# Where a weight piece begins in its buffer, against the activations that stream past it

## The chip, the cores and the metric

One core of a Trainium2 chip runs the whole program. The metric is the time of one execution on the device, in microseconds (us); the smaller the better. TensorE (PE in the profile) does two things for each matmul: it loads a stationary block of 128x128 values (LDWEIGHTS, the row PEld) and then streams the moving operand past it (MATMUL, the row PE). Both operands lie in the on-chip memory SBUF, where each tile has a byte address that is the same in all 128 partitions.

## The reference

Two transformer-like blocks on 256 tokens of width 2048, in float32. The first puts 16 meta tokens ahead, so its first projection works on 272 columns.

```
# first block
proj = rms(h) @ w_in                       # 2048 -> 10704
y_a  = rwkv7(...); y_b = fox_attention(...)
h = h + (g_a * (y_a @ w_a) + g_b * (y_b @ w_b)) @ w_o
h = h + (silu(gate) * up) @ w_down         # gate, up = rms(h) @ w_gate_up, width 5632
# second block
proj = rms(h) @ w_in_2                     # hyena and latent attention
h = h + rms(concat(rms(y_hyena), rms(y_attn)) @ w_out_2)
h = h + rms((gelu(conv3(g)) * u) @ w_down_2)   # g, u = rms(h) @ w_up_2, width 5632
```

## The kernel before

Every dense layer keeps its activations transposed in SBUF, 128 features by 256 (or 272) tokens for each of its k blocks, as two tiles: a high part (`xh`, in the chip's rounded float32 form) and the rest (`xl`). Weights come from memory in **pieces**: 8 blocks of 128x128, 4096 bytes in each partition. `weights` fetches a piece on the SP queue into `wr`, ScalarE writes its high part `wh` (line 191), VectorE the rest `wl` (line 192). `wr`, `wh` and `wl` rotate over three buffers each. `stream` hands out the blocks of a weight matrix piece by piece; `dense` takes one per k block and `mm3` issues three matmuls for it: `wh` by `xh` (L209), `wl` by `xh` (L210), `wh` by `xl` (L211). With a k depth of 16 a result takes two pieces, with 44 (`w_down`) five and a half. Piece numbers below count from 0 within a stream.

A scheduler orders each engine's instructions ahead of time from a simulated timeline; the order is fixed when the program is built. The stages follow each other:

| stage | matmuls stream | us in the profile |
|---|---|---|
| `w_in` with the RWKV and attention heads between | xh, xl | 0 to 801 |
| `w_ab` (`phase_merge`) | yah, yal, ybh, ybl | 801 to 916 |
| `w_o` | mh, ml | 916 to 1017 |
| `w_gu` (`phase_glu`) | x2h, x2l | 1017 to 1504 |
| `w_down` | hh, hl | 1504 to 1753 |
| `w_in2`, `w_q2`, `w_k2`, hyena, attention (`phase_mix`) | x3h, x3l; hyh, hyl; huh, hul | 1753 to 2013 |
| `w_out2` (`phase_out`) | yhh, yhl, yah2, yal2 | 2013 to 2113 |
| `w_up2` (`phase_conv_glu`) | x4h, x4l | 2113 to 2609 |
| `w_down2` (`phase_last`) | the weights, 512 columns at a time | 2609 to 2866 |

From `w_ab` through `w_o` the small matmuls of the hyena filters (dh, dl by flsh, flsl, fldh, fldl) and some float32 ones stand between the dense ones; in `phase_mix` those of hyena and attention do.

**Addresses.** The text speaks of the *distance* of a matmul: the byte address of its weight block less that of the block that it streams, modulo 256. A block of weights is 512 bytes and a block of 256 tokens 1024 bytes, so within a stage the distance is the same for all matmuls of a piece; in `w_in` a block of 272 tokens is 1088 bytes, and the distance goes down by 64 from one k block to the next. The addresses are those of the built program: `wh` at 40736, 44832, 48928 and `wl` at 53024, 57120, 61216 (all 32 modulo 256); xh 106912 (160), yah 65376 (96), mh 180192 (224), x2h, x3h and x4h 65376 (96), hh 122848 (224), yhh 194528 (224). `shift` allocates a tile of 64 bytes that nobody reads, so that the tiles behind it begin 64 bytes later.

Some pieces come apart from the others: `away` names pieces that `stream` puts in a pool of their own (tiles `awh`, `awl`), at another distance: 2, 6, 40 and 100 of `w_gu` and 10, 14, 48 and 100 of `w_up2` have distance 0, and 2 of `w_down` has 128. The filters' matmuls (dh, dl) have distance 0 throughout.

Of the kernel before, what the change touches and what calls it, by code (L numbers as in the profile page):

```python
# [12 lines left out]
F32R = mybir.dt.float32r  # L13
# [5 lines left out]
P = 128  # L19
D = 2048  # L20
KT = D // P
S = 256
# [6 lines left out]
HT = HID // P  # L29
C0 = math.exp(-0.5)  # L30
BIG = 1e30
PIECE = 8


# [48 lines left out]
CML, NCML = layout([("perm", 128), ("cos", S), ("sin", S)])  # L83
# [67 lines left out]
class Builder:  # L151
# [41 lines left out]

    def weights(self, src, kt, pools=None, size=PIECE, tag="w"):

        nc = self.nc
        praw, phi, plo = pools or (self.wraw, self.whi, self.wlo)
        w = self.tl(praw, [P, size, P], "wr")
        wh = self.tl(phi, [P, size, P], tag + "h", F32R)
        wl = self.tl(plo, [P, size, P], tag + "l", F32R)  # L200
        with self.tc.high_priority(offset=2000):
            nc.sync.dma_start(out=w[:, :kt], in_=src)
            self.split(w[:, :kt], wh[:, :kt], wl[:, :kt])
        return wh, wl
# [7 lines left out]

    def shift(self, pool):

        self.tl(pool, [P, 16], "shift")

    def stream(self, name, away=(), pool=None):


        w = self.a[name]  # L220
        for i in range(w.shape[0]):
            if i in away:
                wh, wl = self.weights(w[i], PIECE, (self.wraw, pool[0], pool[0]), tag="aw")
            else:
                wh, wl = self.weights(w[i], PIECE)
            for k in range(PIECE):
                yield wh[:, k], wl[:, k]
# [78 lines left out]
    def run(self):  # L306
# [16 lines left out]
        with ExitStack() as right:  # L323
# [15 lines left out]
            with ExitStack() as pb:  # L339
                xp = self.pool(pb, "x2")  # L340
                self.shift(xp)
                xh = self.tl(xp, [P, KT, S], "x2h", F32R)
                xl = self.tl(xp, [P, KT, S], "x2l", F32R)
                st = self.stream("w_o")
                for i in range(KT):
                    ps = self.bank()
                    self.dense(ps, st, KT, mh, ml, al)
                    self.residual(i, ps, "n2", xh, xl)
                    next(filters, None)
                pf.close()  # L350
                pm.close()
                self.rstd(self.R[:, :S], self.total(self.acc), S, 1.0 / D, 1e-6)
                self.dump("h1", self.h)
                pd = ExitStack()
                hp = self.pool(pd, "hp", side="right")
                hh = self.tl(hp, [P, HT, S], "hh", F32R)
                hl = self.tl(hp, [P, HT, S], "hl", F32R)
                self.phase_glu(xh, xl, hh, hl)
            with ExitStack() as pc:
                xp = self.pool(pc, "x3")  # L360
                self.shift(xp)
                xh = self.tl(xp, [P, KT, S], "x3h", F32R)
                xl = self.tl(xp, [P, KT, S], "x3l", F32R)
                with ExitStack() as c:
                    st = self.stream("w_down", (2,), [self.pool(c, "pdn")])
                    for i in range(KT):
                        ps = self.bank()
                        self.dense(ps, st, HT, hh, hl, al)
                        self.residual(i, ps, "pre", xh, xl)
                        if i % 4 == 3:  # L370
                            nc.scalar.dma_start(out=spill[:, i - 3 : i + 1], in_=self.h[:, i - 3 : i + 1])
                pd.close()
                self.dump("h2", self.h)
                ph.close()
                self.rstd(self.R[:, :S], self.total(self.acc), S, 1.0 / D, 1e-6)
                py = ExitStack()
                yp = self.pool(py, "yp", side="right")
                ys = [self.tl(yp, [P, 8, S], n, F32R) for n in ("yhh", "yhl", "yah2", "yal2")]
                rs = [self.tl(yp, [P, S], n) for n in ("Rh", "Ra")]
                self.phase_mix(xh, xl, ys, rs)  # L380
            with ExitStack() as pe:
                xp = self.pool(pe, "x4")
                self.shift(xp)
# [12 lines left out]
                self.phase_conv_glu(xh, xl, hh, hl, bring, spill2, pf)  # L396
                self.dump("h3", self.h)
# [111 lines left out]
    def phase_merge(self, pa, mh, ml, filters):  # L509
        nc, a = self.nc, self.a  # L510
        al = slice(0, S)
        w = self.pool(pa, "pmgy")
        self.shift(w)
        w2 = self.pool(pa, "pmg", 2)
# [4 lines left out]
        for j, k in ((0, 2), (2, 2), (4, 2), (6, 2)):  # L519
            for sp, yh, yl in ys:  # L520
                y = self.tl(w, [P, 2, S], "yraw", bufs=2)
                with self.tc.high_priority(offset=1500):
                    nc.gpsimd.dma_start(out=y, in_=sp[j : j + k].rearrange("j p s -> p j s"))
                    self.split(y, yh[:, j : j + k], yl[:, j : j + k])
        st = self.stream("w_ab")
        self.banks = "dac"
# [20 lines left out]
    def phase_glu(self, xh, xl, hh, hl):  # L547
# [3 lines left out]
        with ExitStack() as c:  # L551
            st = self.stream("w_gu", (2, 6, 40, 100), [self.pool(c, "pgl")])
            w2 = self.pool(c, "pglu", 2)
            for i in range(HT):
                ps = self.bank()
# [24 lines left out]
    def phase_mix(self, xh, xl, ys, rs):  # L580
# [3 lines left out]
        with ExitStack() as c:  # L584
# [7 lines left out]

            win2 = self.stream("w_in2")

# [53 lines left out]
            for q in range(2):  # L648
                wh, wl = self.weights(a["w_v2"][q], PIECE)
                wh, wl = (x.rearrange("p (k x) c -> p k (x c)", k=2) for x in (wh, wl))  # L650
                for b in range(2):
# [6 lines left out]
                    nc.scalar.copy(vt[:, b, 512 * q : 512 * q + 512], ps)  # L658
            acca = self.tl(w, [P, S], "acca")
            acch = self.tl(w, [P, S], "acch")  # L660
            hyena = self.hyena(w, w2, inproj, ys, acch)
            for h in range(8):
# [13 lines left out]
                for b in range(2):  # L676
                    nc.vector.tensor_scalar(out=sc[:, b], in0=sc[:, b], scalar1=sm[:, b : b + 1], scalar2=None, op0=ALU.mult)
                    for s_ in range(2):
                        nc.tensor.transpose(pT[:, s_, b], sc[:, b, 128 * s_ : 128 * s_ + 128], self.con("ident"))
                pt = self.tl(w, [P, 2, 2, P], "mpt")  # L680
                nc.scalar.copy(pt, pT)
# [191 lines left out]
    def phase_conv_glu(self, xh, xl, hh, hl, bring, spill, pf):  # L873
# [3 lines left out]
        with ExitStack() as c:  # L877
            pool = []
            st = self.stream("w_up2", (10, 14, 48, 100), pool)
            first = [self.bank() for _ in range(4)]  # L880
# [4 lines left out]
            pf.close()  # L885
            pool.append(self.pool(c, "pcgw"))
            w2 = self.pool(c, "pcg", 2)
# [68 lines left out]
    def phase_x(self, pa):  # L956
# [4 lines left out]
        with ExitStack() as ph:  # L961
# [55 lines left out]
    def phase_heads(self):  # L1017
# [5 lines left out]
        with ExitStack() as pr:  # L1023
# [46 lines left out]
            self.fox_setup(pr)  # L1070
            self.pgate = self.pool(pr, "pgate", 1)
            for j in range(9):
# [337 lines left out]
```

## Time and profile before

| | |
|---|---|
| median of 3 runs | 2872.4 us (2871.46 to 2873.11) |
| the profiled execution, its own time | 2867.63 us |
| its span | 2865.8 us |
| granted TensorE clock, mean | 0.994 |
| PE busy | 2827.8 us, 99% of the span |
| DVE (VectorE) busy | 1852.2 us, 65% |
| ACT (ScalarE) busy | 1340.8 us, 47% |

A row of the timeline gives the start of an instruction and how long it took; matmuls overlap, so what each costs is the step from one start to the next. A row of the windows gives, for a stretch, its length, PE's busy time, how many PE instructions touch it, the granted clock, and the DMA share and rate; length by count is the step, where the stretch holds one kind of matmul (the count takes in the one or two that reach over its ends).

### The profile page before, as it was taken

The numbers are of one execution on the slowest core, as the hardware profiler recorded it, in microseconds if no ns is written. First come the engines' busy times: TensorE is split into PE (matmuls) and PEld (weight loads), VectorE is DVE, ScalarE is ACT, GpSimd is POOL, SyncE is SP. The second block draws the span as 40 slices with busy tenths as digits, with TensorE's granted clock in tenths as the row PEclk, the third lists the DMA queues.
The fourth block names the chain that finished last, engine by engine and source line by source line (L and its number), as shares of the span: only waits on it lengthen the run. The fifth ranks groups of instructions, "written<-read, shape, count | busy, mean of one in ns | idle before, by whom it ended". The sixth has DMA issues, their size and how long they took to land.

```text
span 2865.8 us, 56247 instructions
## 1 busy us (share of the span) xinstructions
PE 2827.8 (99%) x23286; PEld 2664.8 (93%) x23286; DVE 1852.2 (65%) x2948; ACT 1340.8 (47%) x1998; POOL 184.8 (6%) x339
## 2 busy tenths in 40 slices
PE   8999999999999999999999999999989999999998
PEld 7988888888999999999999999999989999999886
DVE  8856676676566665555655556777787666775444
ACT  6544555555444454444444445544454444444443
POOL 4000000001000200000000000001120000000000
PEclk9999999999999999999999999999999999999999
DMA  6433333333576555555555556444555555556554
GB/s 211 136 108 112 107 113 110 109 104 129 186 237 208 188 187 193 187 185 193 196 193 193 197 192 220 162 147 146 192 179 191 191 187 190 194 196 228 191 191 162
DMA packets 147617, 497.23 MB, mean 174 GB/s; under 512 B 16224, under 2 KB 30816, under 8 KB 146784
## 3 DMA queue, kind: packets, MB, share of 16 engines
q1 hardware_dynamic: 128448, 458.42, 48.5%
q10 hardware_dynamic: 18272, 33.12, 3.4%
q8 instruction: 182, 2.98, 0.4%
q0 software_dynamic: 640, 2.10, 0.3%
q14 instruction: 75, 0.61, 0.1%
HBM read 478.37 MB, written 15.20 MB: 172 GB/s over the span
## 4 chain that ended last, share of the span: by engine, by line
PE 95%; DVE 2%; DMA 1%; ACT 1%; issue 0%; SPq 0%; POOL 0%; ACTq 0%; DVEq 0%; POOLq 0%
PE psd L211 12%; PE psd L210 12%; PE psd L209 12%; PE psb L209 5%; PE psb L211 5%; PE psb L210 5%; PE psa L211 5%; PE psc L210 5%; PE psa L210 5%; PE psa L209 4%; PE psc L209 4%; PE psc L211 4%; PE psa L937 1%; PE psd L938 1%; PE psd L937 1%; PE psa L938 1%
## 5 line engine op out<-in xcount | busy, mean ns | idle before, releaser
L192 DVE TENSOR_TENSOR wl<-wr,wh 128x1024 fp32r<-128x1024 f32 (+1 forms) x863 | 1055.1, 1223 | 642.8 <-ACT wh L191 641.5
L191 ACT CAST wh<-wr 128x1024 fp32r<-128x1024 f32 (+1 forms) x863 | 900.9, 1045 | 1199.0 <-PE psd L211 345.4
L210 PE MATMUL psd<-xh,wl 128*128 128x256 f32 (+2 forms) x1280 | 371.6, 290 | 0.7 <-DVE wl L192 0.7
L211 PE MATMUL psd<-xl,wh 128*128 128x256 f32 (+2 forms) x1280 | 371.4, 290 | 0.0
L209 PE MATMUL psd<-xh,wh 128*128 128x256 f32 (+2 forms) x1280 | 369.9, 289 | 0.6 <-DVE p L1011 0.6
L209 PEld LDWEIGHTS psd<-xh,wh 128*128 128x128 f32 x1280 | 241.2, 188 | 8.6 <-issue 4.1
L211 PEld LDWEIGHTS psd<-xl,wh 128*128 128x128 f32 x1280 | 241.1, 188 | 7.8 <-issue 3.2
L210 PEld LDWEIGHTS psd<-xh,wl 128*128 128x128 f32 x1280 | 240.9, 188 | 6.1 <-DVE wl L192 0.9
L209 PE MATMUL psd<-x3h,wh 128*128 128x256 f32 x496 | 140.5, 283 | 0.0
L211 PE MATMUL psd<-x3l,wh 128*128 128x256 f32 x496 | 140.4, 283 | 0.0
L210 PE MATMUL psd<-x3h,wl 128*128 128x256 f32 x496 | 138.8, 280 | 0.0
L260 POOL TENSOR_TENSOR acc<-acc,ssq 128x256 f32<-128x256 f32 x56 | 72.1, 1287 | 858.9 <-ACT ssq L262 858.8
L209 PE MATMUL psa<-x4h,wh 128*128 128x256 f32 x344 | 96.0, 279 | 4.2 <-ACT x4h L250 4.2
L210 PE MATMUL psa<-x4h,wl 128*128 128x256 f32 x344 | 96.1, 279 | 2.9 <-DVE wl L192 2.9
L211 PE MATMUL psa<-x4l,wh 128*128 128x256 f32 x344 | 96.4, 280 | 1.2 <-DVE x4l L251 0.8
L209 PEld LDWEIGHTS psd<-x3h,wh 128*128 128x128 f32 x496 | 93.2, 188 | 2.7 <-ACT huh L191 1.3
L209 PE MATMUL psa<-x2h,wh 128*128 128x256 f32 x344 | 95.6, 278 | 0.0
L210 PE MATMUL psb<-x4h,wl 128*128 128x256 f32 x344 | 95.6, 278 | 0.0
L211 PE MATMUL psa<-x2l,wh 128*128 128x256 f32 x344 | 95.5, 278 | 0.0
L210 PE MATMUL psd<-x4h,wl 128*128 128x256 f32 x344 | 95.5, 278 | 0.0
L210 PE MATMUL psc<-x4h,wl 128*128 128x256 f32 x344 | 95.5, 278 | 0.0
L210 PE MATMUL psa<-x2h,wl 128*128 128x256 f32 x344 | 95.5, 278 | 0.0
(720 smaller groups left out, 8503.4 us busy)
## 6 DMA issues: line engine op xcount, KB each, us to landing
wr<-w_in_dram SPq DMA_DIRECT2D x230, 512.0 KB, 3.4
wr<-w_gu_dram SPq DMA_DIRECT2D x176, 512.0 KB, 3.3
wr<-w_down_dram SPq DMA_DIRECT2D x176, 512.0 KB, 3.4
wr<-w_up_dram SPq DMA_DIRECT2D x176, 512.0 KB, 3.5
wr<-w_ab_dram SPq DMA_DIRECT2D x32, 512.0 KB, 4.2
wr<-w_o_dram SPq DMA_DIRECT2D x32, 512.0 KB, 3.4
wr<-w_out_dram SPq DMA_DIRECT2D x32, 512.0 KB, 4.3
spill_g<-gate ACTq DMA_DIRECT2D x32, 128.0 KB, 3.0
```

The lines of the kernel that those rows point to most:

```text
L191: self.nc.scalar.copy(hi, src)
L192: self.nc.vector.tensor_tensor(out=lo, in0=src, in1=hi.bitcast(F32), op=ALU.subtract)
L209: nc.tensor.matmul(out, lhsT=wh, rhs=xh, start=start, stop=False)
L210: nc.tensor.matmul(out, lhsT=wl, rhs=xh, start=False, stop=False)
L211: nc.tensor.matmul(out, lhsT=wh, rhs=xl, start=False, stop=stop)
L260: nc.gpsimd.tensor_tensor(out=acc, in0=acc, in1=self.pending[id(acc)], op=ALU.add)
L937: nc.tensor.matmul(ps[b], lhsT=hh[:, k, bs], rhs=wl[:, q], start=False, stop=False)
L938: nc.tensor.matmul(ps[b], lhsT=hl[:, k, bs], rhs=wh[:, q], start=False, stop=k == HT - 1)
```

## The change

The tiles `wh` and `wl` become rooms of 4608 bytes, and a piece begins in its room at a word that the stage chooses (`off`, in words of 4 bytes). The idle `shift` tiles go, and so do the pools for the pieces apart: those pieces now lie in the same rooms, 48 words further (modulo 64). In `w_in` the blocks of a piece stand 144 words apart (`pitch`) instead of 128, which is 576 bytes, so that their addresses advance as the 272-token blocks do, modulo 256.

```diff
+ROOM = PIECE * (P + 16)
-    def weights(self, src, kt, pools=None, size=PIECE, tag="w"):
+    def weights(self, src, kt, pools=None, size=PIECE, tag="w", off=0, pitch=P):
...
-        wh = self.tl(phi, [P, size, P], tag + "h", F32R)
-        wl = self.tl(plo, [P, size, P], tag + "l", F32R)
+        if pools:
+            wh, wl = (self.tl(p, [P, size, P], tag + q, F32R) for p, q in ((phi, "h"), (plo, "l")))
+        else:
+            wh, wl = (self.tl(p, [P, ROOM], tag + q, F32R) for p, q in ((phi, "h"), (plo, "l")))
+            at = 0 if pitch > P else off
+            wh, wl = (x[:, at : at + size * pitch].rearrange("p (k c) -> p k c", k=size) for x in (wh, wl))
+            wh, wl = (x[:, :, off - at : off - at + P] for x in (wh, wl))
...
-    def stream(self, name, away=(), pool=None):
+    def stream(self, name, off=0, away=(), pitch=P):
         w = self.a[name]
         for i in range(w.shape[0]):
-            if i in away:
-                wh, wl = self.weights(w[i], PIECE, (self.wraw, pool[0], pool[0]), tag="aw")
-            else:
-                wh, wl = self.weights(w[i], PIECE)
+            o = off(i) if callable(off) else off
+            wh, wl = self.weights(w[i], PIECE, off=(o + 48) % 64 if i in away else o, pitch=pitch)
...
-                self.shift(xp)
-                st = self.stream("w_o")
+                st = self.stream("w_o", 0, (15, 17, 19, 21))
...
-                    st = self.stream("w_down", (2,), [self.pool(c, "pdn")])
+                st = self.stream("w_down", 0, (1, 3, 7, 9))
...
-        st = self.stream("w_ab")
+        st = self.stream("w_ab", 16)
...
-            st = self.stream("w_gu", (2, 6, 40, 100), [self.pool(c, "pgl")])
+            st = self.stream("w_gu", 16, (3, 5, 7, 9))
...
-            win2 = self.stream("w_in2")
+            win2 = self.stream("w_in2", 16)
...
-            acca = self.tl(w, [P, S], "acca")
+            acca = self.tl(w, [P, S], "rq")
...
-                pt = self.tl(w, [P, 2, 2, P], "mpt")
+                pt = self.tl(w, [P, NCML], "cml")[:, : 4 * P].rearrange("p (s b x) -> p s b x", s=2, b=2)
...
-            st = self.stream("w_up2", (10, 14, 48, 100), pool)
+            st = self.stream("w_up2", 16, (11, 13, 15, 17))
...
-            self.win = self.stream("w_in")
+            whole = [k in ("k", "v", "fk", "fv", "wf", "ad") for k, _ in in_order()]
+            self.win = self.stream("w_in", lambda i: 16 if i >= 8 and whole[i // 2] else 0, pitch=P + 16)
...
-        t = self.tl(self.pgate, [P, S], "gate")
+        t = self.acc
```

The distances that the built programs give:

| stage | before | after |
|---|---|---|
| `w_in`, 256 columns | 64, 0, 192, 128 in turn by k block | 64 |
| `w_in`, 272 columns | 128, 64, 0, 192 in turn | 192 |
| `w_in`, 258 columns | 72, 8, 200, 136 in turn | 72 |
| `w_ab` | 192 | 64 |
| `w_o` | 64 | 64; 0 in pieces 15, 17, 19, 21 |
| `w_gu` | 192; 0 in pieces 2, 6, 40, 100 | 64; 0 in pieces 3, 5, 7, 9 |
| `w_down` | 64; 128 in piece 2 | 64; 0 in pieces 1, 3, 7, 9 |
| `w_in2` | 192 | 64 |
| `w_q2`, `w_k2` | 192 | 0 |
| `w_out2` | 64 | 64 |
| `w_up2` | 192; 0 in pieces 10, 14, 48, 100 | 64; 0 in pieces 11, 13, 15, 17 |
| `w_down2` | 192 | 192 |

The order of instructions on each engine stays as it was, but for the pieces apart. On PE four matmuls move: around the pieces 40 and 100 of `w_gu` (and 48 and 100 of `w_up2`) the first matmul of the piece apart stood one ahead of its turn. PE before, around the border of pieces 39 and 40 of `w_gu`, where `awh` is the piece apart and `psa` takes its result:

```order
L211 MATMUL psd_13936<-x2l_11580,wh_13938 128x256
L209 MATMUL psd_13936<-x2h_11579,wh_13968 128x256
L209 MATMUL psa_14002<-x2h_11579,awh_14004 128x256
L210 MATMUL psd_13936<-x2h_11579,wl_13969 128x256
L211 MATMUL psd_13936<-x2l_11580,wh_13968 128x256
```

PE after, at the same place, where piece 40 is one like the others:

```order
L218 MATMUL psd_13895<-x2l_11542,wh_13897 128x256
L216 MATMUL psd_13895<-x2h_11541,wh_13927 128x256
L217 MATMUL psd_13895<-x2h_11541,wl_13928 128x256
L218 MATMUL psd_13895<-x2l_11542,wh_13927 128x256
L216 MATMUL psd_13895<-x2h_11541,wh_13927 128x256
```

The one matmul of distance 0 that stood alone among those of distance 192 is back in its place behind piece 39. On VectorE and ScalarE the splits of the pieces apart stood some rows earlier, since their buffers were free. VectorE before, at the same border (`awl` is the split of piece 40, `wl_13969` that of 39):

```order
L192 TENSOR_TENSOR hl_12695<-glu_u_13867,hh_12694 128x256
L192 TENSOR_TENSOR awl_14005<-wr_14003,awh_14004 128x1024
L192 TENSOR_TENSOR wl_13969<-wr_13967,wh_13968 128x1024
L558 TENSOR_TENSOR glu_g_13933<-psc_13872,R_85 128x256
L192 TENSOR_TENSOR wl_14035<-wr_14033,wh_14034 128x1024
```

VectorE after, the same place:

```order
L193 TENSOR_TENSOR hl_12657<-glu_u_13826,hh_12656 128x256
L193 TENSOR_TENSOR wl_13928<-wr_13926,wh_13927 128x1024
L555 TENSOR_TENSOR glu_g_13892<-psc_13831,R_85 128x256
L193 TENSOR_TENSOR wl_13964<-wr_13962,wh_13963 128x1024
L193 TENSOR_TENSOR wl_13994<-wr_13992,wh_13993 128x1024
```

The split of piece 40 (`wl_13964` now) waits its turn behind that of piece 39 and the gate row. The tiles `gate`, `mpt` and `acca` take the room of `acc`, `cml` and `rq`, whose readers are done by then; the splits of `w_in` write eight blocks 128x8x128 with gaps in place of one run 128x1024.

More of the change, by code (lines that the diff above doesn't have):

```diff
@@ L211, in mm3 @@
         nc.tensor.matmul(out, lhsT=wh, rhs=xl, start=False, stop=stop)
-    def shift(self, pool):
-        self.tl(pool, [P, 16], "shift")
-    def stream(self, name, away=(), pool=None):
+    def stream(self, name, off=0, away=(), pitch=P):
         w = self.a[name]
         for i in range(w.shape[0]):
-            if i in away:
-                wh, wl = self.weights(w[i], PIECE, (self.wraw, pool[0], pool[0]), tag="aw")
-            else:
-                wh, wl = self.weights(w[i], PIECE)
+            o = off(i) if callable(off) else off
+            wh, wl = self.weights(w[i], PIECE, off=(o + 48) % 64 if i in away else o, pitch=pitch)
             for k in range(PIECE):
@@ L360, in run @@
                 xp = self.pool(pc, "x3")
-                self.shift(xp)
                 xh = self.tl(xp, [P, KT, S], "x3h", F32R)
                 xl = self.tl(xp, [P, KT, S], "x3l", F32R)
-                with ExitStack() as c:
-                    st = self.stream("w_down", (2,), [self.pool(c, "pdn")])
[L366 to L371, printed above, removed]
+                st = self.stream("w_down", 0, (1, 3, 7, 9))
+                for i in range(KT):
+                    ps = self.bank()
+                    self.dense(ps, st, HT, hh, hl, al)
+                    self.residual(i, ps, "pre", xh, xl)
+                    if i % 4 == 3:
+                        nc.scalar.dma_start(out=spill[:, i - 3 : i + 1], in_=self.h[:, i - 3 : i + 1])
                 pd.close()
@@ L382, in run @@
                 xp = self.pool(pe, "x4")
-                self.shift(xp)
                 xh = self.tl(xp, [P, KT, S], "x4h", F32R)
@@ L512, in phase_merge @@
         w = self.pool(pa, "pmgy")
-        self.shift(w)
         w2 = self.pool(pa, "pmg", 2)
@@ L877, in phase_conv_glu @@
         with ExitStack() as c:
-            pool = []
-            st = self.stream("w_up2", (10, 14, 48, 100), pool)
+            st = self.stream("w_up2", 16, (11, 13, 15, 17))
             first = [self.bank() for _ in range(4)]
@@ L885, in phase_conv_glu @@
             pf.close()
-            pool.append(self.pool(c, "pcgw"))
             w2 = self.pool(c, "pcg", 2)
@@ L1070, in phase_heads @@
             self.fox_setup(pr)
-            self.pgate = self.pool(pr, "pgate", 1)
             for j in range(9):
```

## The prediction

> **What bounds the kernel.** I read the page first, then windows of the stages, then the timeline of PE at the places where the distance changes. The page:
>
> ```profile
> PE 2827.8 (99%) x23286; PEld 2664.8 (93%) x23286; DVE 1852.2 (65%) x2948; ACT 1340.8 (47%) x1998; POOL 184.8 (6%) x339
> PE 95%; DVE 2%; DMA 1%; ACT 1%; issue 0%; SPq 0%; POOL 0%; ACTq 0%; DVEq 0%; POOLq 0%
> ```
>
> PE is busy for 99% of the span and makes 95% of the chain that ended last. So the step from one matmul to the next is the price of the kernel, nearly everywhere, and the change touches just that. Windows of PE:
>
> ```profile
> 770.60:801.00 30.40, 30.40 (x259) 1.00 0.74 229
> 957.90:1017.30 59.40, 59.40 (x507) 1.00 0.58 194
> 1026.70:1124.90 98.20, 98.20 (x867) 1.00 0.58 189
> 1133.30:1294.30 161.00, 161.00 (x1370) 1.00 0.56 185
> 1300.10:1504.00 203.90, 203.90 (x1802) 1.00 0.58 192
> 1515.40:1752.90 237.50, 237.50 (x2019) 1.00 0.59 191
> 1765.10:1776.10 11.00, 11.00 (x98) 1.00 0.86 289
> 1782.40:1788.00 5.60, 5.60 (x50) 1.00 0.56 190
> 2044.70:2107.00 62.30, 62.30 (x552) 1.00 0.62 201
> 2154.20:2252.40 98.20, 98.20 (x867) 1.00 0.58 192
> 2260.80:2399.30 138.50, 138.50 (x1178) 1.00 0.56 185
> 2405.00:2606.00 201.00, 201.00 (x1776) 1.00 0.58 192
> ```
>
> The granted clock is 1.00 in all, and yet a matmul of one shape has two prices. In 1300.1 to 1504.0 it is 203.9 / 1800 = 113.3 ns, in 1133.3 to 1294.3 it is 161.0 / 1368 = 117.7 ns: the same stage (`w_gu`), the same distance 192. `w_down` at distance 64 goes at 237.5 / 2017 = 117.8 ns throughout, `w_out2` at the same distance 64 at 62.3 / 550 = 113.3 ns. So PE has a **fast** and a **slow** gait, 4.45 ns apart, each keeps itself up for hundreds of matmuls, and both occur at 64 and at 192. The distance alone does not choose: what comes just before does. Two kinds of event switch the gait. The first is a piece at distance 0. Timeline of PE, the end of piece 2 of `w_gu` (distance 0) and the start of piece 3 (192):
>
> ```profile
> 1026.42 0.28 PE L210 MATMUL psb<-x2h,awl 128*128 128x256 f32 x1
> 1026.54 0.28 PE L211 MATMUL psb<-x2l,awh 128*128 128x256 f32 x1
> 1026.66 0.28 PE L209 MATMUL psb<-x2h,wh 128*128 128x256 f32 x1
> 1026.77 0.28 PE L210 MATMUL psb<-x2h,wl 128*128 128x256 f32 x1
> 1026.88 0.28 PE L211 MATMUL psb<-x2l,wh 128*128 128x256 f32 x1
> ```
>
> At distance 0 the step is 120 ns (1026.42, 1026.54, 1026.66), the dearest of all; behind it, at 192, PE goes fast. And this is the end of a run of distance 0 in the filters and the next matmul of `w_o`, at distance **64**:
>
> ```profile
> 926.41 0.28 PE L209 MATMUL psb<-fldh,dh 128*128 128x256 f32 x1
> 926.53 0.28 PE L210 MATMUL psb<-fldh,dl 128*128 128x256 f32 x1
> 926.65 0.28 PE L211 MATMUL psb<-fldl,dh 128*128 128x256 f32 x1
> 926.77 0.28 PE L211 MATMUL psa<-ml,wh 128*128 128x256 f32 x1
> 926.89 0.28 PE L209 MATMUL psa<-mh,wh 128*128 128x256 f32 x1
> 927.01 0.28 PE L210 MATMUL psa<-mh,wl 128*128 128x256 f32 x1
> 927.12 0.28 PE L211 MATMUL psa<-ml,wh 128*128 128x256 f32 x1
> ```
>
> Again 120 ns at 0 (926.41, 926.53, 926.65), but then 117 to 119 ns: slow. The trace has seven exits from three or more matmuls at 0 to distance 64 (919.6 to 953.2 us), and all seven end slow. Of the exits to 192 whose last steps were all 120 ns, five of five end fast. A fast run at 64 is knocked out too, by two matmuls at 0:
>
> ```profile
> 940.67 0.28 PE L210 MATMUL psd<-mh,wl 128*128 128x256 f32 x1
> 940.78 0.28 PE L211 MATMUL psd<-ml,wh 128*128 128x256 f32 x1
> 940.89 0.28 PE L209 MATMUL psb<-flsh,dh 128*128 128x256 f32 x1
> 941.01 0.28 PE L210 MATMUL psb<-flsh,dl 128*128 128x256 f32 x1
> 941.13 0.28 PE L209 MATMUL psd<-mh,wh 128*128 128x256 f32 x1
> 941.25 0.28 PE L210 MATMUL psd<-mh,wl 128*128 128x256 f32 x1
> 941.37 0.28 PE L211 MATMUL psd<-ml,wh 128*128 128x256 f32 x1
> ```
>
> 11 hundredths of a us a step before, 12 after. The second event is a stall, mostly behind a float32 matmul (L746 here):
>
> ```profile
> 934.87 0.38 PE L746 MATMUL psb<-fw,s2x 64*128 64x256 f32 x1
> 935.17 0.39 PE L209 MATMUL psc<-mh,wh 128*128 128x256 f32 x1
> ...
> 935.98 0.28 PE L209 MATMUL psc<-mh,wh 128*128 128x256 f32 x1
> 936.09 0.28 PE L210 MATMUL psc<-mh,wl 128*128 128x256 f32 x1
> ```
>
> At 64, PE comes out of it fast (113 ns); seven of the eight such places with eight clean matmuls behind them do. At 192 only 6 of 52 do: 1782.4 to 1788.0, behind two stalls, is 5.6 / 48 = 117 ns.
>
> **The change, part by part.** The sum is against the profiled execution (2867.6 us); the median of the runs shown is 4.8 us above it, which I add at the end.
>
> *`w_gu`.* Before, pieces 3 to 39 and from 101 on were fast: 865 less 24 at distance 0 in the first window and 1800 in the second, 2641 matmuls in all. After, the distance is 64, the stage opens behind float32 matmuls (so pieces 1 and 2, some 70 matmuls, should be fast), then the level pieces 3, 5, 7 and 9 come, and by the seven exits each leaves PE slow, with no stall behind it to the end of the stage. (2641 - 70) x 4.45 ns = +11.4 us. The four level pieces cost what the four before did.
>
> *`w_up2`.* The same pattern: 841 and (2405.0 to 2606.0) 1774, with some 26 to the end of the piece 2641. Some 260 matmuls at its start follow stalls and may turn fast. (2641 - 260) x 4.45 ns = +10.6 us.
>
> *`w_o` and `w_down`* were slow (59.4 / 505 = 117.6 ns from 957.9 on; 117.8), and stay so; eight level pieces for one at 128 cost 7 x 24 x 2.2 ns = +0.4 us. `w_q2` and `w_k2`, eight pieces, go from 192 to 0: at most 192 x 2.2 ns = +0.4 us.
>
> *`w_ab` and `w_in2`*, which are full of stalls, go from 192 to 64. By the order of the changed program some 1530 of their matmuls have a stall as the last event, not a run at 0; 374 went fast before (96 of them in 1765.1 to 1776.1, at 11.0 / 96 = 114.6 ns with a stall in it). 1156 x 4.45 = -5.1 us if all turn fast, 0 if none does; seven eighths give -4.5.
>
> *`w_in`.* Before, the distance turned with the k block, and its clean end costs 30.4 / 257 = 118.3 ns, slow in effect. After, the weights that load during a k block's third matmul stand one 64 further: 64, 64, 128 for 256 columns and 192, 192, 0 for 272. No stage shows this. Bounds: all 1920 matmuls of 256 columns and 1632 of 272 fast, 3552 x 4.7 = -16.7 us; or one in three of the 272 as dear as at 0, 544 x 2.3 = +1.3 us. The nearest rows are the turning ones, 118.3 ns, so I take -1.
>
> *The rest at nothing.* The splits of `w_in` write with gaps; `gate` waits for its own copy to memory as before:
>
> ```profile
> L192 DVE TENSOR_TENSOR wl<-wr,wh 128x1024 fp32r<-128x1024 f32 (+1 forms) x863 | 1055.1, 1223 | 642.8 <-ACT wh L191 641.5
> L191 ACT CAST wh<-wr 128x1024 fp32r<-128x1024 f32 (+1 forms) x863 | 900.9, 1045 | 1199.0 <-PE psd L211 345.4
> ```
>
> VectorE stands idle 642.8 us ahead of these splits and ScalarE 1199.0 us; that covers 168 pieces at a tenth more, 168 x 0.12 = 20 us, except while the first x blocks come in (at most +1 us). With that cover gone, the splits would be late next. The splits of the former pieces apart are no longer early, and there PE would have 24 matmuls, 2.8 us, before it misses one.
>
> Sum: 11.4 + 10.6 + 0.4 + 0.4 - 4.5 - 1 = **+17.3 us**: 2884.9 on the profiled execution's scale, 2889.7 on the median's. Part of the 4.8 us between them may be that the runs shown were slow in more places than the profile, and then there is less to lose; I take **2888 us**. This case alone spans 2876 (`w_in` gains 10) to 2897.
>
> **Rivals.** *The level pieces work at 64 as at 192.* For it: at 192 they do, five of five. Against it: the seven exits. It decides at the first level piece of `w_gu`, at 64: fast behind it, and all that was slow turns fast: `w_gu` 1480 matmuls, `w_up2` 1450, `w_down` 1990, `w_o` 310, 5230 x 4.45 = -23.3 us, and with the -5.1 of the next-to-last part, 0.8 for level pieces and -1, -28.6: 2844 us.
>
> *Mixed.* One of the two large stages keeps or regains its fast gait, or `w_in` comes near its lower bound: 17.3 - 11 to 17.3 - 22, near 2873, between 2862 and 2879.
>
> *The place of a piece does nothing, and the gait has another cause.* Then the time stays at 2872. The nearest rows speak against it: 120 ns at every run of distance 0, 113 or 118 elsewhere, at one clock. The Trainium skill bears on this: "TensorE: Matmul & The Clock Gate", in "Step-by-step: what each phase is for", says that PE has two independent SBUF read ports and that loading the next weights takes no read bandwidth from the running matmul. By that rule no distance could matter and the sum above would be nothing; the three prices in this trace at a clock of 1.00 don't agree with it.
>
> **How the numbers follow.** Chances: slow behind level pieces 0.63, they work 0.20, mixed 0.11, no effect 0.06. Anything within 0.2% (5.7 us) is no change here. The first case is slower (0.62 of its 0.63), the second faster, the mixed one parts 0.04, 0.03 and 0.04, the last is the same with 0.05. Faster 0.25, same 0.08, slower 0.67. The first case, the mixed one and the last reach 2862 to 2897 and hold about 0.78 of the chance; to leave out no more than 0.2 the range goes down into the second case, to 2843.
>
> **What would show it.** Right: in the windows of `w_gu` and `w_up2` behind their last level piece 117.8 ns a matmul, in `w_down` and `w_o` as well; steps of 117 to 119 ns behind each level piece; in `w_in2` more stretches at 113. Wrong: 113.3 ns behind any level piece at 64; then those stages shrink by 4.45 ns a matmul and the forecast has the wrong sign.

## The result and the profile after

The changed kernel takes 2888.0 us (median of four runs, 2886.32 to 2892.12) against 2871.9 for the kernel before on the same chip: a ratio of 1.0061 (95% interval 1.0043 to 1.0078). It is slower, by 16 us. A second comparison, told below, gave 2890.6 against 2869.2, 1.0081 (1.0063 to 1.0099). The profiled execution of the first took 2892.12 us, its span is 2890.3; the granted clock is 0.994 as before. The lines of the page that answer to those shown of before:

```profile
PE 2850.9 (99%) x23286; PEld 2688.0 (93%) x23286; DVE 1853.8 (64%) x2948; ACT 1339.1 (46%) x1998; POOL 185.6 (6%) x339
PE 96%; DVE 2%; DMA 1%; ACT 1%; issue 0%; SPq 0%; DVEq 0%; POOL 0%; ACTq 0%
```

The number of matmuls is the same, PE is busy 23.1 us longer, and it still makes the chain. Apart from one wait in `w_ab` that grew by 2.2 us (told below) PE waits as before: the matmuls themselves became dearer. Windows of PE (length, busy time and count of PE, then PEld, DVE, ACT, POOL, the granted clock, DMA share and rate), in turn in `w_gu` (three), `w_down`, `w_out2` and `w_up2` (two):

```profile
1046.00:1146.00 100.00, 100.00 (x851) 100.00 (x851) 57.44 (x71) 42.83 (x54) 0.00 (x0) 1.00 0.58 187
1146.00:1346.00 200.00, 200.00 (x1700) 200.00 (x1700) 115.12 (x142) 85.18 (x106) 0.00 (x0) 1.00 0.58 187
1346.00:1512.00 166.00, 166.00 (x1412) 166.00 (x1411) 95.58 (x117) 70.43 (x90) 0.00 (x0) 1.00 0.57 187
1545.00:1755.00 210.00, 210.00 (x1786) 210.00 (x1785) 108.69 (x103) 87.56 (x102) 19.51 (x14) 1.00 0.59 194
2052.00:2110.00 58.00, 58.00 (x495) 58.00 (x494) 38.64 (x54) 25.24 (x32) 13.90 (x10) 1.00 0.61 194
2190.00:2390.00 200.00, 200.00 (x1700) 200.00 (x1699) 136.10 (x193) 85.32 (x107) 2.26 (x35) 1.00 0.57 187
2390.00:2600.00 210.00, 210.00 (x1785) 210.00 (x1784) 143.40 (x205) 89.59 (x112) 2.53 (x38) 1.00 0.57 186
```

Two of each count reach over the ends, so these are 200 / 1698 = 117.8 ns in `w_gu` and in `w_up2`, where before 1800 and 1774 matmuls in a row went at 113.3, all at a clock of 1.00. Timeline of PE where the first level piece of `w_gu` ends (the matmul at 1028.01 is the first whose successor stands at 64):

```profile
1027.65 0.28 PE L218 MATMUL psb<-x2l,wh 128*128 128x256 f32 x1
1027.77 0.28 PE L216 MATMUL psb<-x2h,wh 128*128 128x256 f32 x1
1027.89 0.28 PE L217 MATMUL psb<-x2h,wl 128*128 128x256 f32 x1
1028.01 0.28 PE L218 MATMUL psb<-x2l,wh 128*128 128x256 f32 x1
1028.12 0.28 PE L216 MATMUL psc<-x2h,wh 128*128 128x256 f32 x1
1028.24 0.28 PE L217 MATMUL psc<-x2h,wl 128*128 128x256 f32 x1
1028.36 0.28 PE L218 MATMUL psc<-x2l,wh 128*128 128x256 f32 x1
1028.48 0.28 PE L216 MATMUL psc<-x2h,wh 128*128 128x256 f32 x1
```

Steps of 12 hundredths before the border and 11 to 12 behind it: from level (120.0) to slow (117.8), never to fast. All sixteen level pieces of the four stages end so. But PE was slow ahead of fifteen of them too; only the first of `w_down` found it fast, with steps of 113 ns.

Stage by stage, in us, from the first matmul that streams a stage's activations to the first of the next (`w_up2` with `w_down2`, to PE's last matmul), for the profiles of this study:

| stage | before | after | after, again | far side | near, no level | far, no level | large only |
|---|---|---|---|---|---|---|---|
| `w_in` | 794.8 | 792.4 | 792.9 | 792.0 | 793.1 | 791.7 | 793.5 |
| `w_ab` | 114.9 | 115.8 | 116.4 | 112.9 | 115.5 | 114.3 | 114.2 |
| `w_o` | 100.9 | 101.1 | 101.1 | 99.2 | 100.9 | 98.6 | 99.2 |
| `w_gu` | 486.6 | 498.3 | 498.3 | 480.4 | 498.1 | 498.1 | 480.4 |
| `w_down` | 249.0 | 249.1 | 249.1 | 240.3 | 239.6 | 249.0 | 240.3 |
| `w_in2` | 256.2 | 255.9 | 255.9 | 256.9 | 257.6 | 255.9 | 257.5 |
| `w_out2` | 104.3 | 106.7 | 104.4 | 104.1 | 104.2 | 103.8 | 103.8 |
| `w_up2`, `w_down2` | 740.5 | 752.4 | 752.4 | 737.1 | 752.3 | 752.1 | 735.2 |

The loss is 11.7 us in `w_gu`, 11.9 in `w_up2`, and in this one profile 2.4 in `w_out2`. What the text calls a level run below is a run of matmuls at distance 0; a step is clean when nothing held the matmul up.

### The profile page after: what moved, and what is told of

It is laid out like the page before. It is cut to its first block, busy times and chain, and to the rows that moved or that the text cites. A ratio compares the mean times of both kernels' runs of the same rounds, so it can differ in the third digit from the quotient of the medians.

```text
span 2890.3 us, 56235 instructions
## 1 busy us (share of the span) xinstructions
PE 2850.9 (99%) x23286; PEld 2688.0 (93%) x23286; DVE 1853.8 (64%) x2948; ACT 1339.1 (46%) x1998; POOL 185.6 (6%) x339
## 4 chain that ended last, share of the span: by engine, by line
PE 96%; DVE 2%; DMA 1%; ACT 1%; issue 0%; SPq 0%; DVEq 0%; POOL 0%; ACTq 0%
PE psd L218 12%; PE psd L217 12%; PE psd L216 12%; PE psb L216 5%; PE psb L217 5%; PE psb L218 5%; PE psc L217 5%; PE psa L218 5%; PE psa L217 5%; PE psc L216 5%; PE psc L218 5%; PE psa L216 5%; PE psd L932 1%; PE psa L931 1%; PE psd L931 1%; PE psa L932 1%
## 5 line engine op out<-in xcount | busy, mean ns | idle before, releaser
L193 DVE TENSOR_TENSOR wl<-wr,wh 128x1024 fp32r<-128x1024 f32 (+1 forms) x872 | 1065.8, 1223 | 668.8 <-ACT wh L192 667.7
L216 PE MATMUL psb<-x4h,wh 128*128 128x256 f32 x352 | 99.2, 282 | 0.0
L218 PE MATMUL psb<-x4l,wh 128*128 128x256 f32 x352 | 99.1, 281 | 0.0
L218 PE MATMUL psd<-x4l,wh 128*128 128x256 f32 x352 | 99.0, 281 | 0.0
L216 PE MATMUL psc<-x4h,wh 128*128 128x256 f32 x352 | 99.0, 281 | 0.0
```

The costliest lines, as they stand in the source:

```text
L193: self.nc.vector.tensor_tensor(out=lo, in0=src, in1=hi.bitcast(F32), op=ALU.subtract)
L216: nc.tensor.matmul(out, lhsT=wh, rhs=xh, start=start, stop=False)
L218: nc.tensor.matmul(out, lhsT=wh, rhs=xl, start=False, stop=stop)
```

## The experiments

The theory is that of the prediction: PE has a fast and a slow gait, and the side on which a stage stands decides in which of them a level piece leaves it. The rivals: level pieces do nothing reliable; 192 is fast by itself; the place has no effect.

**Far side.** The changed kernel, with the four large dense stages at 192:

```diff
-wh, wl = self.weights(w[i], PIECE, off=(o + 48) % 64 if i in away else o, pitch=pitch)
+wh, wl = self.weights(w[i], PIECE, off=(o + 16) % 64 if i in away else o, pitch=pitch)
-self.stream("w_o", 0, (15, 17, 19, 21))
+self.stream("w_o", 32, (15, 17, 19, 21))
-self.stream("w_down", 0, (1, 3, 7, 9))
+self.stream("w_down", 32, (1, 3, 7, 9))
-self.stream("w_gu", 16, (3, 5, 7, 9))
+self.stream("w_gu", 48, (3, 5, 7, 9))
-self.stream("w_up2", 16, (11, 13, 15, 17))
+self.stream("w_up2", 48, (11, 13, 15, 17))
```

> The changed kernel with one edit: in w_o, w_gu, w_down and w_up2 the pieces stand at distance 192 instead of 64; the same pieces stay level (distance 0). Theory 1 (the side decides: out of a level run PE goes slow at 64 and fast at 192): behind the first level piece all four stages go at 113.3 ns instead of 117.8; about 3960 matmuls of w_gu, 3750 of w_up2, 1990 of w_down and 310 to 600 of w_o, some 10150 x 4.45 ns = 45 us less than the changed kernel, so 2843 us (2838 to 2850). Rival A (level pieces are without reliable effect, the gait is set by stalls and by chance): at most a few us from the changed kernel's 2888. Rival B (the place of a piece does nothing): 2888 within 0.2%.

Measured: 2843.5 us (2842.28 to 2845.44), 0.9909 of before (0.9893 to 0.9926). Windows in `w_gu`, `w_down` and `w_up2`:

```profile
1253.00:1490.00 237.00, 237.00 (x2094) 237.00 (x2093) 141.56 (x174) 105.31 (x132) 0.00 (x0) 1.00 0.61 194
1520.00:1730.00 210.00, 210.00 (x1856) 210.00 (x1855) 112.07 (x105) 91.48 (x106) 19.57 (x14) 1.00 0.62 201
2340.00:2560.00 220.00, 220.00 (x1944) 220.00 (x1943) 156.44 (x223) 97.16 (x122) 2.79 (x42) 1.00 0.59 194
```

237 / 2092, 210 / 1854 and 220 / 1942 are all 113.3 ns. The same level pieces that left PE slow at 64 leave it fast at 192, and moving four stages by 128 bytes is worth some 44 us: 17.9 + 8.8 + 15.3 + 1.9 = 43.9 in the stage times. Both "no reliable effect" and "the place does nothing" fall.

**Without level pieces, on either side.** Two kernels; the edit is the same in both, on the changed kernel and on the far side one:

```diff
-self.stream("w_gu", 16, (3, 5, 7, 9))
+self.stream("w_gu", 16)
...
```

> The changed kernel without any level piece in w_o, w_gu, w_down and w_up2; all stay at distance 64. Theory 1 (a gait keeps itself up until an event; level pieces at 64 knock it to slow): w_gu enters behind float32 matmuls as it did in the changed kernel, slow, and stays slow, which changes its time by four pieces x 24 x 2.2 ns = -0.2 us; w_down came in fast (113.3 ns up to its first level piece) and now has nothing to knock it out, so 1990 x 4.45 = -8.9 us there; w_o and w_up2 enter as before, slow, or fast where a stall at their start leaves them so. Total near 2878, and w_down alone decides: 113.3 ns to its end. Rival A (gait lost by chance after some hundred matmuls): w_down at 117.8 for its larger part, total 2885 to 2889. Rival C (at 64 the slow gait always comes back by itself within a piece or two): w_down slow from its second piece on, 2887.

> The four stages at distance 192, without any level piece. Theory 1 (distance alone gives nothing; the level piece makes the switch): w_gu and w_up2 come out of their float32 matmuls and stalls slow (at 192 only 6 of 52 such places ended fast before) and stay slow for the whole stage, 117.8 ns; w_down and w_o by how they enter, a gain of at most 8.9 and 2 us. So 2877 to 2889. Rival D (192 is fast by itself, level pieces are not needed): all four stages at 113.3 ns, 2840 to 2845, as fast as with level pieces or half a us faster.

Measured at 64: 2878.4 us (median of ten runs, 2861.08 to 2882.14). Windows in `w_gu`, `w_down`, `w_up2`:

```profile
1300.00:1510.00 210.00, 210.00 (x1786) 210.00 (x1785) 121.29 (x150) 89.80 (x112) 0.00 (x0) 1.00 0.57 186
1520.00:1752.00 232.00, 232.00 (x2049) 232.00 (x2049) 122.66 (x116) 100.64 (x116) 19.56 (x14) 1.00 0.61 200
2400.00:2600.00 200.00, 200.00 (x1701) 200.00 (x1700) 136.21 (x195) 85.42 (x106) 2.38 (x36) 1.00 0.57 187
```

`w_down` came in fast and stays so to its end (232 / 2047 = 113.3 ns); its level pieces were what made it slow, and taking them away gives 9.5 us. The other two stay slow and take as long as with level pieces (498.1 us for 498.3, 752.3 for 752.4): at 64 the level pieces did not make these two slow, they only did not make them fast, which they do at 192. Measured at 192: 2885.1 us (2883.49 to 2889.98). The same stages:

```profile
1300.00:1508.00 208.00, 208.00 (x1768) 208.00 (x1768) 119.21 (x147) 88.93 (x111) 0.00 (x0) 1.00 0.57 186
1520.00:1755.00 235.00, 235.00 (x1998) 235.00 (x1997) 120.55 (x114) 97.76 (x113) 19.55 (x14) 1.00 0.59 194
2400.00:2600.00 200.00, 200.00 (x1701) 200.00 (x1700) 136.85 (x197) 84.99 (x106) 2.25 (x34) 1.00 0.57 187
```

All at 117.8 ns (235 / 1996 in `w_down`): 192 is not fast by itself, and that rival falls. Only `w_o` is fast there (98.6 us), behind the filters' own level runs. At 192 the level piece makes the switch to fast; at 64 it makes the switch to slow where PE came fast, as in `w_down`.

**First ladder.** In one kernel many distances one after the other:

```diff
+GU = (64, 192, 32, 224, 96, 160, 128, 16, 240, 8, 248)
+UP = ((192, 64), (192, 128), (192, 32), (192, 224), (192, 96), (192, 160), (64, 192), (64, 128), (64, 224), (64, 160))
+DN = (0, 8, 248, 16, 240, 32, 224, 128, 96, 160, 192)
+def at_gu(i): return (0 if i % 16 < 2 else GU[i // 16]) // 4
...
-self.stream("w_gu", 16, (3, 5, 7, 9))
+self.stream("w_gu", at_gu)
...
```

> An instrument, read by its windows and not by its time. In w_gu each group of 16 pieces opens with two level pieces and goes on with 14 pieces at one distance: 64, 192, 32, 224, 96, 160, 128, 16, 240, 8, 248 in turn. In w_up2, from piece 16 on, each group of 16 opens with two level pieces, then four pieces at a first distance and ten at a second: 192 then 64, 128, 32, 224, 96, 160; then 64 followed by 192, 128, 224, 160. In w_down each group of 8 is level, 64, 64, one piece at a trial distance (0, 8, 248, 16, 240, 32, 224, 128, 96, 160, 192), then four pieces at 192. Theory 1 (side): groups of w_gu at 32, 64, 96 go at 117.8 ns, those at 160, 192, 224 at 113.3; a gait once taken is kept over a step to another distance that is not close to 0, so w_up2 stays at 113.3 after 192 and at 117.8 after 64; in w_down only the trial at 0, and perhaps those within 16 of it, make the 192 behind them fast. Rival B: every group at the same step, whatever its distance. Rival E (each distance has its own gait, history does not count): in w_up2 the second distance alone sets the step, the same as in w_gu's group of that distance.

Windows in the eleven groups of `w_gu`, in the order of `GU`:

```profile
1030.00:1060.00 30.00, 30.00 (x257) 30.00 (x256) 16.98 (x21) 12.47 (x16) 0.00 (x0) 1.00 0.55 182
1072.00:1102.00 30.00, 30.00 (x267) 30.00 (x266) 18.41 (x24) 13.23 (x17) 0.00 (x0) 1.00 0.60 195
1116.00:1146.00 30.00, 30.00 (x256) 30.00 (x255) 17.81 (x22) 12.04 (x15) 0.00 (x0) 1.00 0.56 188
1160.00:1190.00 30.00, 30.00 (x259) 30.00 (x259) 17.27 (x22) 13.12 (x16) 0.00 (x0) 1.00 0.57 185
1206.00:1236.00 30.00, 30.00 (x258) 30.00 (x257) 17.89 (x22) 12.36 (x16) 0.00 (x0) 1.00 0.59 191
1252.00:1282.00 30.00, 30.00 (x252) 30.00 (x252) 17.49 (x22) 12.04 (x15) 0.00 (x0) 1.00 0.56 185
1298.00:1328.00 30.00, 30.00 (x256) 30.00 (x255) 17.69 (x23) 12.16 (x16) 0.00 (x0) 1.00 0.57 186
1344.00:1374.00 30.00, 30.00 (x255) 30.00 (x255) 17.58 (x23) 12.61 (x16) 0.00 (x0) 1.00 0.57 182
1390.00:1420.00 30.00, 30.00 (x252) 30.00 (x251) 17.12 (x23) 12.66 (x16) 0.00 (x0) 1.00 0.54 178
1436.00:1466.00 30.00, 30.00 (x262) 30.00 (x261) 17.81 (x24) 13.43 (x17) 0.00 (x0) 1.00 0.57 190
1480.00:1510.00 30.00, 30.00 (x258) 30.00 (x257) 17.74 (x23) 12.69 (x16) 0.00 (x0) 1.00 0.55 183
```

One matmul more or less in such a window is half a ns; the starts of the second half of each group give the finer mean:

| distance | 0 | 8 | 16 | 32 | 64 | 96 | 128 | 160 | 192 | 224 | 240 | 248 |
|---|---|---|---|---|---|---|---|---|---|---|---|---|
| step, ns | 120.0 | 115.6 | 118.3 | 118.3 | 117.8 | 117.3 | 118.7 | 120.0 | 113.3 | 116.7 | 120.0 | 117.6 |

So the theory's wording, "the side", was wrong: 160 and 240 lie on the same side as 192 and are as dear as level. Rival B (every group the same) is far off. In `w_up2`, behind four pieces at the other of the two, PE at 64 (first row) and at 192 (second):

```profile
2194.00:2219.00 25.00, 25.00 (x223) 25.00 (x222) 18.07 (x27) 11.26 (x14) 0.40 (x6) 1.00 0.58 190
2464.00:2489.00 25.00, 25.00 (x215) 25.00 (x213) 17.45 (x25) 10.30 (x14) 0.40 (x6) 1.00 0.56 188
```

25 / 221 = 113 ns at 64 behind the fast gait, 25 / 213 = 117 at 192 behind the slow one: the gait is carried over from 64 to 192 and back. At 128, 224 and 160 the step was the same behind either gait (118.7, 116.7 and 120.0), so there rival E holds: the distance alone sets it. At 96 a trial of 24 matmuls in `w_down` went at 120.1, the two long groups at 117.3, so it may have two as well. Of the trials in `w_down`, 0, 32, 96 and 160 left PE fast at 192, the others slow; ahead of 32, 96 and 128 PE was fast already, ahead of the rest slow. Theory 1 gave this to 0 and perhaps its neighbours within 16 alone, so it missed here too: 8, 16, 240 and 248 switched nothing, and 160 did. And three of the eleven level pieces there left PE **fast** at 64. The starts of one such place:

```profile
1630.00 0.28 PE L238 MATMUL psd<-hh,wl 128*128 128x256 f32 x1
1630.11 0.29 PE L239 MATMUL psd<-hl,wh 128*128 128x256 f32 x1
1630.23 0.28 PE L237 MATMUL psd<-hh,wh 128*128 128x256 f32 x1
1630.35 0.29 PE L238 MATMUL psd<-hh,wl 128*128 128x256 f32 x1
1630.48 0.28 PE L239 MATMUL psd<-hl,wh 128*128 128x256 f32 x1
1630.60 0.28 PE L237 MATMUL psd<-hh,wh 128*128 128x256 f32 x1
1630.72 0.28 PE L238 MATMUL psd<-hh,wl 128*128 128x256 f32 x1
1630.83 0.28 PE L239 MATMUL psd<-hl,wh 128*128 128x256 f32 x1
1630.94 0.28 PE L237 MATMUL psd<-hh,wh 128*128 128x256 f32 x1
```

The last level steps are 117, 121, 120, 124 ns, a wave, where the others end on steady steps of 119 to 121. Counted over all ten profiles, with those of before and of the kernels below (level runs of 18 matmuls or more, with 20 behind them that nothing held up):

| last four level steps | 64 behind it | 192 behind it |
|---|---|---|
| all 119 to 121 (settled) | slow 93 of 93 | fast 69 of 69 |
| a wave | fast 3 of 3 | slow 7 of 7 |

A level run of 18 or more thus has two forms, and in these counts the form together with the distance goes with the gait behind it; the row of the wave at 64 rests on three runs of one execution. Shorter runs do not keep to the table. Behind the filters' runs of twelve in `w_ab`, settled by the same rule, PE stayed fast at 64 in 16 of 16 places (eight profiles), where it had been fast before; behind the same runs in `w_o` it was slow at 64 in 10 of 10, where it had been slow before. The end of one of the 16, in the profile of after:

```profile
877.99 0.28 PE L217 MATMUL psb<-fldh,dl 128*128 128x256 f32 x1
878.11 0.28 PE L218 MATMUL psb<-fldl,dh 128*128 128x256 f32 x1
878.23 0.28 PE L217 MATMUL psc<-yah,wl 128*128 128x256 f32 x1
...
878.81 0.28 PE L216 MATMUL psc<-yah,wh 128*128 128x256 f32 x1
878.93 0.28 PE L217 MATMUL psc<-yah,wl 128*128 128x256 f32 x1
879.04 0.28 PE L218 MATMUL psc<-yal,wh 128*128 128x256 f32 x1
```

Whether the length of the run or what stands beside it makes the difference was not tried. The table also shows why one level piece may not do: in the far side kernel the first one of `w_gu` was a wave and left PE slow, and the second put it right.

**Large only.** The far side kernel with `w_in`, `w_ab` and `w_in2` at the distances of the kernel before:

```diff
-self.stream("w_ab", 16)
+self.stream("w_ab", 48)
-self.stream("w_in2", 16)
+self.stream("w_in2", 48)
-self.stream("w_in", lambda i: 16 if i >= 8 and whole[i // 2] else 0, pitch=P + 16)
+self.stream("w_in")
```

> The kernel of e1_far_side with w_in, w_ab and w_in2 put back to the distances of the kernel before (w_in: blocks of a piece 128 words apart; w_ab and w_in2 at 192); the level pieces and the 192 of w_o, w_gu, w_down and w_up2 stay. Theory 1 (in the stages full of waits a fast matmul only lengthens the next wait): w_in back to some 794.8 us (2.0 to 3.1 more than in the four profiles since the change), but PE then waits that much less for the filter weights in w_ab, and w_in2 stays at 256 us, so the sum of the three stages is within 1.5 us of that of e1_far_side (1161.8 us) and the time is 2843 (2840 to 2847). Rival A (the 64 of those stages is worth what I put on it, 4.5 + 1 us, and more for w_in): 2848 to 2850.

Measured: 2847.9 us (2844.63 to 2852.56), 0.9926 of before (0.9910 to 0.9943). The three stages sum to 1165.2 us in its profile against 1161.8: 3.4 us, where I allowed 1.5. Rival A is nearer, 2848. But the intervals of the two kernels overlap, and the same sum differs as much between profiles that share their distances: 1164.1 and 1165.2 in the two of the changed kernel, 1166.2 and 1161.9 in the two without level pieces, and 1165.9 before. What the three stages gain is not settled by one profile of each kernel. In `w_in2` fast matmuls rose from 68 to 577 for 0.6 us: the clean steps there are 2.2 us less and the steps over stalls 1.6 us more, of it one wait of 1.7 us for `yy` on VectorE. There, waits do take most of it.

**Second ladder.** On the far side kernel; `w_gu` tries level runs of one and of two pieces, and `w_down2` several distances:

```diff
+LAST = (192, 64, 128, 0, 64, 0, 192, 96, 160, 32, 224)
+def at_gu(i):
+    n = 1 if i < 88 else 2
+    d = (0, 0, 64, 192, 0) + (0,) * (n - 1) + (64,) * (4 - n)
+    return d[i % 8] // 4
...
-self.weights(a["w_down2"][22 * g + i], PIECE)
+self.weights(a["w_down2"][22 * g + i], PIECE, off=at_last(22 * g + i))
...
-self.stream("w_in", lambda i: 16 if i >= 8 and whole[i // 2] else 0, pitch=P + 16)
+self.stream("w_in", lambda i: 16 if i >= 8 and i // 6 % 2 else 0, pitch=P + 16)
```

> An instrument on the kernel of e1_far_side, read by its windows. w_gu in groups of 8 pieces: two level, one at 64, one at 192, then one level piece (first 11 groups) or two (last 11), and 64 to the group's end. Theory 1a (a level run that has settled to steady steps of 120 leaves PE slow at 64; one that has not settled may leave it fast): behind two level pieces 11 of 11 slow, 117.8 ns; behind one level piece some of 11 fast, 113.3, and those are the groups whose last level steps are not all 119 to 121. Rival F (the exit at 64 is chance whatever the level run does): about as many fast groups in either half. In w_in the columns go by three at a time at two places 64 apart: 64, 64, 128 or 128, 128, 192 for 256 columns (128, 128, 192 or 192, 192, 0 for 272). By the steps of the first ladder (64 at 113 or 118, 128 at 118.7, 192 at 113 or 118, 0 at 120) the two ways come out within 1.5 ns a matmul of each other. In w_down2, where the weights stream 512 columns at a time, groups of 8 pieces at 192, 64, 128, 0, 64, 0, 192, 96, 160, 32, 224. Theory 1: steps differ by distance there too, with at least 3 ns between the best and the worst, and 0 is the worst (228.9 ns at 192 so far). Rival B (with 512 columns a weight load has time enough, the place does not matter): 228.9 ns in all groups, within 0.5.

In `w_gu` all 44 exits to 64 were slow, behind one level piece as behind two; every one of these level runs had settled, so the fast ones I expected did not come. A chance of three in eleven, as in `w_down` of the first ladder, would hardly leave 44 of 44 slow, so rival F has little left; what an unsettled run does at 64 was not tried again. In `w_in` the two places gave 117.6 and 117.3 ns for 256 columns, 125.3 and 124.9 for 272. In `w_down2` the groups came out at 229 (192), 233 (64), 232 (128), **227 (0)**, 233, 227, 229, 234 (96), 233 (160), 233 (32) and 233 ns (224). The distance counts with 512 columns too, but level is the best there, the reverse of what I expected.

**Level last.** The far side kernel with `w_down2` level:

```diff
-self.weights(a["w_down2"][22 * g + i], PIECE)
+self.weights(a["w_down2"][22 * g + i], PIECE, off=48)
```

> The kernel of e1_far_side with one edit: in w_down2, where weights stream 512 columns at a time past a block of activations, the pieces stand level with the blocks (distance 0) instead of at 192. The second ladder gave 227.0 ns a matmul there at 0 against 229.0 at 192; 1056 matmuls x 2.0 ns = 2.1 us. Theory 1 (the distance sets the step with 512 columns as well, and the best place is another one): w_down2 at 227 ns throughout, 2841.4 us (2840 to 2843.5), and the remaining stages as in e1_far_side. Rival G (the ladder's 227 hung on what came before it there): 229 ns and more, 2843.5 or above.

Measured: 2841.8 us (2839.9 to 2843.78), 0.9903 of before (0.9888 to 0.9918); the interval overlaps that of the far side, but the stage shows it. A window in `w_down2` of the far side kernel, and the same of this one:

```profile
2620.00:2700.00 80.00, 80.00 (x351) 65.65 (x350) 37.13 (x32) 33.11 (x36) 0.00 (x0) 1.00 0.59 192
2620.00:2700.00 80.00, 80.00 (x354) 66.24 (x354) 36.85 (x32) 33.92 (x36) 0.00 (x0) 1.00 0.59 192
```

349 matmuls against 352 in 80 us; the starts give 228.9 and 226.7 ns, 1056 x 2.2 = 2.3 us. By its median this is the fastest version of the study, 27 us below the kernel before.

**Again.** The changed kernel as it is, for a second profile (no edit).

> The changed kernel once more, as it is, for a second profile of it. Theory 1: w_gu and w_up2 slow throughout again (117.8 ns), since their level pieces settle every time; w_out2, which has no level piece and turned slow behind a wait in the first profile (106.7 us), is a matter of how PE comes out of that wait and goes fast here, 104 us, as in the kernel before and in the three kernels that share its distance. Time 2885 to 2889 us. Rival (the slow w_out2 belongs to the changed kernel): 106 to 107 us again.

Measured: 2890.6 us (2889.71 to 2898.84), 1.6 us above the range given. `w_gu` and `w_up2` are slow again, to a tenth of a us. `w_out2`, in the first profile (above, 58 / 493 = 117.6 ns) and here:

```profile
2056.00:2112.00 56.00, 56.00 (x497) 56.00 (x495) 38.30 (x52) 25.32 (x31) 15.17 (x11) 1.00 0.63 201
```

56 / 495 = 113.1 ns: the slow `w_out2` was that execution's, not the change's.

## Why the prediction was right, and where it was not

It said 2888 us, and 2888.0 and 2890.6 were measured. Its main step held: behind every level piece at 64 PE was slow, so the 2641 matmuls in each of `w_gu` and `w_up2` that a level piece had made fast at 192 were slow. What it rested on was weaker than it looked. In all seven exits PE had been slow ahead of the run (steps of 117 to 120 ns), so they could not show that a level run knocks a fast PE out; only the run of two did, and the filters' runs of twelve in `w_ab` did not do so after the change. And the way into slow was another one in the large stages: they were slow ahead of their first level piece, and in the profile without level pieces they stay as slow. Of the four stages with level pieces the knock-out itself shows in `w_down` alone (249.1 us with level pieces, 239.6 without), which the prediction took for slow anyway. Point by point, on the scale of the two profiles (+24.5 us, where the prediction's sum was +17.3):

- `w_gu`, +11.4 forecast, +11.7 measured. The 70 matmuls that were to be fast at the start were slow: the two float32 matmuls there (steps of 305 ns) left PE slow at 64. The eight places that spoke for fast had steps of 180 to 227 ns over the stall, a shorter kind. `w_up2`, +10.6 forecast, +11.9 measured, is the same: some 60 matmuls of the stage went fast, where I counted on some 260 at its start.
- `w_o` and `w_down`, +0.4 forecast, +0.3 measured.
- `w_ab` and `w_in2` (with `w_q2` and `w_k2`), -4.5 + 0.4 forecast, +0.9 and -0.3 measured. Two terms failed. "Seven eighths" came from those eight places; in the profile after, over all stages at 64, 31 of 58 stalls with eight clean matmuls behind them ended fast, 26 of 43 where that step took 190 to 232 ns and 4 of 14 where it took 295 to 312 (one was of neither kind). Some 450 matmuls more than before went fast, not 1011, and these did count: the clean steps of the two stages are 1.2 and 1.0 us less. The other term stood at nothing: in `w_ab` PE waits for the filters' weights from memory. What `fw` waited for, first before and then after:

```profile
  DMA fw<-filt_dram: 4.3, 1
  DMA fw<-filt_dram: 6.5, 1
```

  PE came to that wait 2.5 us earlier (827.7 for 830.2 us) and the weights only 0.4 us earlier (834.4 for 834.8), so the wait grew by some 2 us. From the start of `w_ab` to the wait PE took 28.5 us in both, so what the wait ate is the lead that `w_in` had won. The transfer was issued 2.5 us earlier as well (818.2 for 820.7) but took 16.1 us for 14.0; it took 14.2 in the far side kernel, where that lead was kept, and 13.2 to 16.3 in the ten profiles of this study. Why is open.
- `w_in`, -1 forecast, -2.4 and -1.9 measured, within the bounds. Where three steps in a row are clean they average 125.0 ns for 272 columns (125.7 before) and 117.9 for 256 (118.0): 1632 x 0.7 + 1920 x 0.1 = 1.3 us. The rest is not shown to be the distance: back at the distances of before, `w_in` took 793.5 us in the large only kernel, not 794.8.
- `w_out2`, nothing forecast, +2.4 in one execution and +0.1 in the other.
- The 4.8 us that I added from the profile to the median: the profile of after is 4.1 us above its own median, that of before 4.3 below. So part of the agreement is luck: the sum fell 7.2 us short in the profiles, and the two profiled executions lie on opposite sides of their medians.

The rival that level pieces work at 64 as at 192 is refuted by the sixteen level pieces of the changed kernel; its 2844 us were reached, at 192. The one by which the place does nothing is refuted by the ladder, twelve distances with steps from 113.3 to 120.0 ns at one clock. The Trainium skill, "TensorE: Matmul & The Clock Gate", section "Step-by-step: what each phase is for", says that loading the next weights takes no read bandwidth from the running matmul. The ladder shows that the place of the weights against what streams counts all the same, 113.3 to 120.0 ns; whether a read port is the reason no run shows.

What stays open: why 64 and 192 have two gaits and the other distances that were tried on both sides have one; what decides whether a level run settles or becomes a wave; why the filters' shorter runs in `w_ab` leave a fast PE fast; and how a stall's length sets the gait. Nor was it profiled why, without level pieces at 64, two of ten executions took 2861.1 and 2864.7 us and the rest 2877 to 2882. A gap of 14 to 17 us is near what one large stage gains when it turns fast (4221 x 4.45 = 18.8), which is an argument and not shown. With level pieces at 192 four executions lay within 3.2 us.

## What to carry to other kernels

Where PE is busy throughout and its clock is full, compare the step of one matmul shape from stage to stage: two prices at one clock pointed to the addresses of the operands here. Before a place is chosen, step through the distances in one run, and through the way into them as well, since the same place may have two gaits; a piece that resets the gait is worth its price only in front of the distance that it makes fast. In stages full of waits, first look at which transfer ends the next wait: here the landing of one transfer moved by 3 us between profiles, more than the faster steps gained, and more than one profile of each kernel is needed to tell them apart.

## What had not been expected of the hardware

- The step of a 128x256 matmul in this kernel goes from 113.3 to 120.0 ns with the distance of its operands modulo 256, and not in order of distance: 8 bytes off gives 115.6, 16 gives 118.3, 160 is as dear as 0.
- A level run of 18 matmuls or more has two forms with nearly one price (120.0 and 120.3 ns), and opposite gaits follow them: at 192 fast in 69 of 69 and slow in 7 of 7. Runs of twelve do not all follow this.
- With 512 streamed columns level is the best place (226.7 ns against 228.9 at 192 and up to 234 elsewhere).
